# RWKV token-mix projections prepared one stream ahead, the gate as split products, and attention heads alternated on halves of the array

## The chip, the cores and the metric

One core of a Trainium2 chip runs the whole program. The metric is the device time of one execution in microseconds. Each version is run several times, and the median is compared. One execution of each is also recorded by the hardware profiler, and its trace is what the rows below come from.

## What is computed

The program is a block of a diffusion backbone over 512 latent and 256 context tokens, 1,024 channels wide. Two of its parts matter here. The first mixes tokens by neighbourhood attention, 64 channels a head:

```python
s_nb = einsum('bchd,bicjhd->bhcij', q_row, k_nb) * scale + bias
s_cx = einsum('bchd,bnhd->bhcn', q_row, k_ctx) * scale
p = softmax(concatenate([s_nb.reshape(...), s_cx], axis=-1), axis=-1)
...
return einsum('bhcij,bicjhd->bchd', p_nb, v_nb) + einsum('bhcn,bnhd->bchd', p[..., n_win:], v_ctx)
```

Context tokens attend to context tokens alone (`context_attention`). The second prepares an RWKV recurrence. Six streams are made of the tokens and of the mean of their neighbours, each by its own `mu`, and each has its own product:

```python
def rwkv_prepare(h, mu, w_rkv, w0, w1, w2, a0, a1, a2, g1, g2, k_k, k_a):
    xx = centred_shift(h) - h                 # 0.5 * (left + right) - h
    xr, xw, xk, xv, xa, xg = h[None] + xx[None] * mu[:, None, None, :]
    r, k, v = einsum('sbtd,sde->sbte', stack([xr, xk, xv]), w_rkv)
    w_logit = w0 + einsum(tanh(einsum('btd,zdr->zbtr', xw, w1)), w2)
    a = sigmoid(a0 + einsum(einsum('btd,zdr->zbtr', xa, a1), a2))
    g = sigmoid(xg @ g1) @ g2
    kk = k * k_k, each head divided by its norm
```

## The kernel before

Activations lie with channels on partitions: eight tiles of 128 channels by 768 tokens (512 latent, then 256 context). Large products run in float32r. `split` (L471) makes of a float32 tile a rounded part on ACT (L473) and the rest of it by a subtraction (L474, on DVE for activations, on POOL for weights, from `load_w`, L476). `dense` (L486, matmul at L495) then multiplies three pairs of parts for each of the eight input tiles k: hi·hi, hi weight by lo activation, lo weight by hi activation. A product of one block of 128 outputs is thus 24 matmuls of 512 columns and, where context is needed, 24 of 256. `dense_pair` (L499) interleaves the first two output blocks over k, so that a stream that is still being made feeds two blocks.

Every engine runs its instructions in one fixed order. A scheduler settles these orders when the program is built, from the order of the code, the data and the release of buffers. [...]

Attention (`na_attn`, L803) is a generator whose steps a written order (`AB_ORDER`) puts between dense products of the same mixer. One call does two heads, which lie on rows 0–63 and 64–127 of the same q and k tiles. It goes over six query blocks i (four latent ones against 512 keys, two context ones against 256) and, within each, over the two heads `hh`: the scores of a unit two further on (L820, L821), softmax (bias and maximum L778, L780, L781; exponent on ACT L785; L786, L787), transposes (L793) with a copy (L798), and the products with values `po` (L842), 64 columns of the array a head. Score, transpose and `po` banks come from one ring of four PSUM banks.

`rw_mixer` (L1105) makes the shifted tiles in `shift` (L1131: scaling on DVE L1135, bias on ACT L1137, the sum of neighbours on POOL L1138, two edge columns on POOL L1139, L1140). `stream(i, parts)` (L1144) makes all eight split tiles of stream i at once: xs (L1155), then `split`; for the first stream it also turns the neighbours' sum into xx, in place (L1151). Its tiles `ah`, `al` have eight buffers each, as many as one stream needs. `project` (L1161) does the products; `keep` (L1171) copies a result out on ACT (L1173) and writes it by DMA; `unit` (L1188) forms the normed k: a product `ssk` (L1192), a root on ACT (L1193), and on DVE L1194, a reciprocal (L1195) and L1196. The streams follow one another as k (2), v (3), w1 (1), a1 (4), r (0) and g1 (5); r and g1 have latent columns alone, w1 and a1 one output block, g1 two. After g1 come a sigmoid (L1227) and the gate: eight blocks of two float32 matmuls (L1230 with 128 rows, L1231 with 32 rows). Behind it the recurrence starts.

## Time and profile before

| | us |
|---|---|
| runs shown | 3583.0, 3583.03, 3589.97 |
| median | 3583.03 |
| the profiled execution, its own time | 3583.87 |
| its span, first to last instruction | 3581.7 |
| PE busy in the span | 3238.9 (90%) |
| DVE, ACT, POOL busy | 1791.7 (50%), 1312.9 (37%), 908.3 (25%) |
| mean granted clock of TensorE, share of full | 0.956 |

PE is the matrix engine, PEld its weight loads (they overlap it), DVE, ACT and POOL the vector, scalar and general engines, SP the engine that issues most DMAs. A busy share is an average over stages. What a change in one stage is worth is read from the rows of that stage. In a row of the timeline, the number behind an engine and line is a group of equal instructions (x8), `128*64` is the rows and columns of the array that a matmul uses, and a bracket gives the idle time before the group and what ended it. A float32 matmul leaves two records, a float32r one leaves one.

### The profile page before, as it was taken

To read this page: it belongs to the slowest core of one execution; us is meant where nothing else is said; L and a number is where in the kernel's file an instruction comes from. 1 tells how busy PE (TensorE), PEld (TensorE's weight loads), DVE (VectorE), ACT (ScalarE), POOL (GpSimd) and SP (SyncE) were. 2 spreads that over 40 slices of the span, in tenths; PEclk is the share of its full clock that TensorE was granted. 3 is DMA by queue.
4 is the path that set the end of the run, shared out by engine and by line. 5 is a ranking of instruction groups with operands and counts; after the bars stand their busy time and mean duration, and the time that the engine had idled before them with its cause. 6 is when DMAs were issued, how large, how long until landed. Compare 5 with 4: busy or idle time off the path is not lost. (4 is left out here: it accounts for less than half of the span.)

```text
span 3581.7 us, 56701 instructions
## 1 busy us (share of the span) xinstructions
PE 3238.9 (90%) x23582; PEld 2448.4 (68%) x23582; DVE 1791.7 (50%) x3066; ACT 1312.9 (37%) x2491; POOL 908.3 (25%) x468
## 2 busy tenths in 40 slices
PE   7999999999999798779999998899999989799887
PEld 4766887788888576467777776677778767433333
DVE  5475564862322655377777674574333564221213
ACT  3232353221212324367777775322233453200001
POOL 1111113322223522432222220444452333200000
PEclk9999999999999898789999999999999999899999
DMA  5212212552122232210000102475331236699997
GB/s 217 94 66 88 83 67 76 195 192 65 59 65 90 88 113 76 69 31 29 27 27 27 31 8 77 139 231 175 94 126 62 66 92 222 254 426 426 426 427 324
DMA packets 126225, 488.05 MB, mean 136 GB/s; under 512 B 13360, under 2 KB 23024, under 8 KB 101648
## 3 DMA queue, kind: packets, MB, share of 16 engines
q1 hardware_dynamic: 119840, 476.86, 36.9%
q8 instruction: 186, 3.05, 0.4%
q10 hardware_dynamic: 4944, 3.36, 0.3%
q0 software_dynamic: 1184, 4.20, 0.3%
q14 instruction: 71, 0.58, 0.0%
HBM read 455.53 MB, written 28.84 MB: 135 GB/s over the span
## 5 line engine op out<-in xcount | busy, mean ns | idle before, releaser
L474 POOL TENSOR_TENSOR wl<-w,wh 128x1024 fp32r<-128x1024 f32 (+1 forms) x258 | 616.8, 2393 | 1640.7 <-ACT wh L473 1444.6
L473 ACT ACTIVATE wh<-w 128x1024 fp32r<-128x1024 f32 (+1 forms) x258 | 265.9, 1032 | 944.1 <-PE dn L495 334.5
L495 PE MATMUL dn<-hh,wh 128*128 128x512 f32 (+1 forms) x768 | 236.1, 362 | 14.2 <-ACT hh L473 14.2
L495 PE MATMUL up<-ah,wl 128*128 128x512 f32 (+1 forms) x768 | 236.7, 363 | 6.4 <-POOL wl L474 6.3
L495 PE MATMUL up<-ah,wh 128*128 128x512 f32 (+1 forms) x768 | 236.9, 364 | 5.7 <-ACT ah L578 2.8
L495 PE MATMUL dn<-hl,wh 128*128 128x512 f32 (+1 forms) x768 | 236.4, 362 | 1.9 <-DVE hl L474 1.9
L495 PE MATMUL up<-al,wh 128*128 128x512 f32 (+1 forms) x768 | 236.5, 362 | 0.2 <-DVE al L579 0.2
L495 PE MATMUL dn<-hh,wl 128*128 128x512 f32 (+1 forms) x768 | 235.5, 361 | 0.9 <-POOL wl L474 0.9
L462 DVE SCALAR_TENSOR_TENSOR side<-wside,condb 128x1024 f32<-128x1024 f32 x128 | 191.9, 1499 | 67.6 <-DMA wside<-ada 66.3
L618 DVE TENSOR_TENSOR u<-u 128x768 f32<-128x768 f32 (+1 forms) x64 | 126.7, 1982 | 132.2 <-ACT u L617 132.2
L586 DVE SCALAR_TENSOR_TENSOR x<-dn,ada,x 128x512 f32<-128x512 f32 x96 | 60.5, 658 | 259.0 <-PE dn L495 259.0
L495 PEld LDWEIGHTS dn<-hh,wh 128*128 128x128 f32 x768 | 128.3, 190 | 39.8 <-ACT hh L473 15.8
L495 PEld LDWEIGHTS up<-ah,wl 128*128 128x128 f32 x768 | 128.5, 190 | 33.4 <-POOL wl L474 10.1
L495 PEld LDWEIGHTS up<-ah,wh 128*128 128x128 f32 x768 | 128.9, 191 | 31.4 <-ACT ah L578 3.9
L495 PEld LDWEIGHTS dn<-hl,wh 128*128 128x128 f32 x768 | 128.1, 190 | 27.4 <-DVE hl L474 3.8
L495 PEld LDWEIGHTS up<-al,wh 128*128 128x128 f32 x768 | 129.0, 191 | 25.2 <-DVE al L579 1.4
L495 PEld LDWEIGHTS dn<-hh,wl 128*128 128x128 f32 x768 | 128.2, 190 | 25.2 <-POOL wl L474 1.7
L495 PE MATMUL rp<-xh,wh 128*128 128x512 f32 x368 | 111.1, 373 | 23.3 <-ACT xh L473 21.5
L495 PE MATMUL rp<-xl,wh 128*128 128x512 f32 x368 | 113.5, 373 | 18.0 <-DVE xl L474 18.0
L473 ACT ACTIVATE hh<-u 128x768 fp32r<-128x768 f32 (+1 forms) x64 | 47.3, 739 | 219.4 <-DVE u L618 219.4
L495 PE MATMUL p<-ah,wh 128*128 128x512 f32 (+1 forms) x320 | 117.0, 394 | 2.2 <-ACT ah L578 1.2
L495 PE MATMUL p<-ah,wl 128*128 128x512 f32 x320 | 113.3, 383 | 2.1 <-POOL wl L474 2.1
(616 smaller groups left out, 7496.7 us busy)
## 6 DMA issues: line engine op xcount, KB each, us to landing
w<-mlp SPq DMA_DIRECT2D x128, 512.0 KB, 3.6
wside<-ada SPq DMA_DIRECT2D x96, 512.0 KB, 4.0
ew<-e_gate SPq DMA_DIRECT2D x45, 1024.0 KB, 19.5
ew<-e_up SPq DMA_DIRECT2D x41, 1024.0 KB, 20.7
ew<-e_down SPq DMA_DIRECT2D x39, 1024.0 KB, 19.5
wada<-ada SPq DMA_DIRECT2D x48, 512.0 KB, 3.8
ewm<-e_up SPq DMA_DIRECT2D x18, 1024.0 KB, 19.6
ewm<-e_down SPq DMA_DIRECT2D x18, 1024.0 KB, 19.6
```

Source lines behind the costliest of these rows:

```text
L462: nc.vector.scalar_tensor_tensor(o, w, 1.0, cb[:, q, :], op0=ALU.mult, op1=ALU.mult, accum_out=out[:, f, q:q + 1])
L473: nc.scalar.activation(hi, src, AF.Copy)
L474: (eng or nc.vector).tensor_tensor(lo, src, hi.bitcast(F32), op=ALU.subtract)
L495: nc.tensor.matmul(ps[:, a:b], ww[:, 128 * k:128 * k + 128], aa[:, a:b], start=(first and k == 0 and q == 0), stop=(last and k == nk - 1 a ...
L586: self.nc.vector.scalar_tensor_tensor(x[:, a:b], ps[:, a:b], gt[:, f, q:q + 1], x[:, a:b], op0=ALU.mult, op1=ALU.add)
L618: nc.vector.tensor_tensor(u[:, lo:hi], u[:, lo:hi], u[:, lo:hi], op=ALU.mult)
```

## The change

**Streams.** `stream` becomes a generator `tiles` in an object `Stream`. `ah` and `al` get 14 buffers (`NX`), so up to six tiles of the next stream can exist beside the eight of the present one. `ahead()` makes one of them behind each product but the first of a long stream; ahead of w1 and a1, which have one product, six tiles of the stream that follows are made in one go. w1 now follows k and precedes v. For the first stream xx is not written: ACT makes h·(1−mu) and DVE adds mu/2 times the neighbours' sum; the writing of xx is moved to the second stream. The first tile's neighbours' sum goes from POOL to DVE.

**Gate.** The sigmoid's result is split; `g2` is loaded and split like other weights. The 32 last rows are stacked three times, so that one matmul of 96 rows does their three products. Each block of the gate is four float32r matmuls in place of two float32 ones.

**Attention.** The scores of both heads of a query block are issued alternately, as are their `po` products, and the scores of the next block go between the two transposes.

```diff
-    o["rw_g1"] = chunk_w(v["rw_g1"][0])
-    o["rw_g2"] = np.ascontiguousarray(v["rw_g2"][0])
+    g1, g2 = v["rw_g1"][0], v["rw_g2"][0]
+    o["rw_g1"] = chunk_w(np.concatenate([g1] + [g1[:, 128:]] * 2, 1))
+    o["rw_g2"] = np.stack([g2[:128], np.concatenate([g2[128:]] * 3 + [np.zeros((32, D), g2.dtype)])])
+NX = 14
...
+                def scores(i):
+                    s = [self.bank("s"), self.bank("s")]
+                    for j in range(2 if i < 4 else 1):
+                        for hh in range(2):
+                            r = slice(64 * hh, 64 * hh + 64)
+                            a = 128 * i if i < 4 else T + 128 * (i - 4)
+                            kj = k[r, 8 * win[i]:8 * win[i] + 256] if i < 4 and j == 0 else k[r, T:]
+                            nc.tensor.matmul(s[hh][:, 256 * j:256 * j + 256], q[r, a:a + 128], kj, start=True, stop=True)
+                    return s
+                s = scores(0)
+                for i in range(6):
+                    pT, s2 = [], None
+                    for hh in range(2):
+                        if i < 4:
+                            pr, w = softmax(s[hh], bias[hh][:, i, :], 512), 512
+                            vs = (win[i] // 8, win[i] // 8 + 2, 7, 8)
+                        else:
+                            pr, w = softmax(s[hh], None, 256), 256
+                            vs = (7, 8)
+                        if hh and i < 5:
+                            s2 = scores(i + 1)
+                        pT.append(p_t(pr, w))
+                        if hh == 0:
+                            yield
+                    s = s2
+                    po = self.bank("po")
+                    for j, v in enumerate(vs):
+                        for hh in range(2):
+                            r = slice(64 * hh, 64 * hh + 64)
+                            nc.tensor.matmul(po[r, :128], vt[:, v, r], pT[hh][:, 128 * j:128 * j + 128],
+                                             start=(j == 0), stop=(j == len(vs) - 1))
                     if i < 4:
...
                         nc.vector.tensor_copy(
                             cat[f][:, :T].rearrange("p (r c) -> p c r", r=8)[:, 16 * i:16 * i + 16, :],
                             po[:, :128].rearrange("p (c r) -> p c r", r=8))
...
+                    else:
                         a = T + 128 * (i - 4)
                         nc.scalar.activation(cat[f][:, a:a + 128], po[:, :128], AF.Copy)
                     yield
@@ -1135,28 +1138,51 @@
                         nc.vector.scalar_tensor_tensor(h[:, a:b], self.x[k][:, a:b], sc[:, k, q:q + 1], r[q],
                                                        op0=ALU.mult, op1=ALU.mult)
                         nc.scalar.activation(h[:, a:b], h[:, a:b], AF.Identity, bias=sh[:, k, q:q + 1])
-                        nc.gpsimd.tensor_tensor(s[:, a + 1:b - 1], h[:, a:b - 2], h[:, a + 2:b], op=ALU.add)
+                        (nc.gpsimd if k else nc.vector).tensor_tensor(s[:, a + 1:b - 1], h[:, a:b - 2], h[:, a + 2:b], op=ALU.add)
                         nc.gpsimd.tensor_copy(s[:, a:a + 1], h[:, a + 1:a + 2])
                         nc.gpsimd.tensor_copy(s[:, b - 1:b], h[:, b - 2:b - 1])
-                def stream(i, parts):
+                m2 = pool.tile([128, 2, 8], F32, name="mu2", bufs=1)
+                nc.vector.tensor_scalar(m2[:, 0, :], self.p("mu")[:, 16:24], 0.5, None, op0=ALU.mult)
+                nc.vector.tensor_scalar(m2[:, 1, :], self.p("mu")[:, 16:24], -1.0, 1.0, op0=ALU.mult, op1=ALU.add)
+                def tiles(i, parts, out):
                     lo, hi = parts[0][0], parts[-1][1]
-                    out = []
                     for k in range(KD):
                         while len(xx) < min(k + 3, KD):
                             shift(len(xx))
+                        t = pool.tile([128, TT], F32, tag="tmp", name=self.uid("xs"), bufs=self.tb)
+                        h = pool.tile([128, TT], F32R, tag="ah", name=self.uid("xh"), bufs=NX)
+                        l = pool.tile([128, TT], F32R, tag="al", name=self.uid("xl"), bufs=NX)
+                        base, mu = hs[k], self.p("mu")[:, 8 * i + k:8 * i + k + 1]
                         if i == 2:
+                            nc.scalar.activation(t, hs[k], AF.Copy, scale=m2[:, 1, k:k + 1])
+                            base, mu = t, m2[:, 0, k:k + 1]
+                        elif i == 1:
                             nc.vector.scalar_tensor_tensor(xx[k], xx[k], 0.5, hs[k], op0=ALU.mult, op1=ALU.subtract)
-                        t = pool.tile([128, TT], F32, tag="tmp", name=self.uid("xs"), bufs=self.tb)
-                        h = pool.tile([128, TT], F32R, tag="ah", name=self.uid("xh"), bufs=KD)
-                        l = pool.tile([128, TT], F32R, tag="al", name=self.uid("xl"), bufs=KD)
-                        nc.vector.scalar_tensor_tensor(t[:, lo:hi], xx[k][:, lo:hi], self.p("mu")[:, 8 * i + k:8 * i + k + 1],
-                                                       hs[k][:, lo:hi], op0=ALU.mult, op1=ALU.add)
+                        nc.vector.scalar_tensor_tensor(t[:, lo:hi], xx[k][:, lo:hi], mu, base[:, lo:hi],
+                                                       op0=ALU.mult, op1=ALU.add)
                         self.split(t[:, lo:hi], h[:, lo:hi], l[:, lo:hi])
                         out.append((h, l))
-                    return out
+                        yield
+                class Stream:
+                    def __init__(st, i, parts):
+                        st.act = []
+                        st.gen = tiles(i, parts, st.act)
+                    def step(st, n=KD):
+                        for _ in range(n):
+                            next(st.gen, None)
+                        return st.act
+                    def ahead(st):
+                        if len(st.act) < NX - KD:
+                            st.step(1)
-                act = stream(2, PARTS)
+                streams = {i: Stream(i, LAT if i in (0, 5) else PARTS) for i in (2, 1, 3, 4, 0, 5)}
+                act = streams[2].step()
                 self.x = None
                 def unit(f, t, sq):
                     for a, b in PARTS:
@@ -1204,31 +1232,52 @@
                     if late:
                         late()
                     late = partial(unit, f, t, sq)
-                act = stream(3, PARTS)
+                    if f > 0:
+                        streams[1].ahead()
+                act = streams[1].step()
+                streams[3].step(NX - KD)
+                for f, ps in project(act, self.i["rw_w1"], 1, PARTS):
+                    factors(tw, ps, AF.Tanh)
+                act = streams[3].step()
+                late()
                 for f, ps in project(act, self.i["rw_v"], KD, PARTS):
                     keep("v", f, ps, 0, TT)
-                    if late:
-                        late = late()
-                act = stream(1, PARTS)
-                for f, ps in project(act, self.i["rw_w1"], 1, PARTS):
-                    factors(tw, ps, AF.Tanh)
-                act = stream(4, PARTS)
+                    if f > 0:
+                        streams[4].ahead()
+                act = streams[4].step()
+                streams[0].step(NX - KD)
                 for f, ps in project(act, self.i["rw_a1"], 1, PARTS):
                     factors(ta, ps, AF.Copy)
-                act = stream(0, LAT)
+                act = streams[0].step()
                 for f, ps in project(act, self.i["rw_r"], KD, LAT):
                     keep("r", f, ps, 0, T)
-                act = stream(5, LAT)
-                tg = pool.tile([128, 2, T], F32, name="tg", bufs=1)
-                g2 = pool.tile([128, 2, D], F32, name="g2", bufs=1)
-                nc.sync.dma_start(g2[:, 0, :], self.i["rw_g2"][:128])
-                nc.sync.dma_start(g2[:32, 1, :], self.i["rw_g2"][128:])
+                    if f > 0:
+                        streams[5].ahead()
+                act = streams[5].step()
+                def part(tag):
+                    return pool.tile([128, TT], F32R, tag=tag, name=self.uid("tg"), bufs=NX)[:, :T]
+                th, tl, tx = part("ah"), part("al"), part("ah")
                 for f, ps in project(act, self.i["rw_g1"], 2, LAT):
-                    nc.scalar.activation(tg[:, f, :], ps[:, :T], AF.Sigmoid)
+                    t = pool.tile([128, TT], F32, tag="tmp", name=self.uid("tg"), bufs=self.tb)[:, :T]
+                    nc.scalar.activation(t, ps[:, :T], AF.Sigmoid)
+                    if f == 0:
+                        self.split(t, th, tl)
+                    else:
+                        nc.scalar.activation(tx[:96], t[:96], AF.Copy)
+                        nc.vector.tensor_tensor(tx[32:64], t[32:64], tx[32:64].bitcast(F32), op=ALU.subtract)
+                g2 = self.load_w(self.i["rw_g2"][0], D)
+                w = self.wraw.tile([128, D], F32, tag="wraw", name=self.uid("w"))
+                nc.sync.dma_start(w, self.i["rw_g2"][1])
+                gx = self.wspl.tile([128, D], F32R, tag="wh", name=self.uid("wh"))
+                nc.scalar.activation(gx[:96], w[:96], AF.Copy)
+                nc.vector.tensor_tensor(gx[64:96], w[64:96], gx[64:96].bitcast(F32), op=ALU.subtract)
                 for f in range(KD):
                     pg = self.bank("g")
-                    nc.tensor.matmul(pg, g2[:, 0, 128 * f:128 * f + 128], tg[:, 0, :], start=True, stop=False)
-                    nc.tensor.matmul(pg, g2[:32, 1, 128 * f:128 * f + 128], tg[:32, 1, :], start=False, stop=True)
+                    c = slice(128 * f, 128 * f + 128)
+                    for n, (w, t) in enumerate(((g2[0], th), (g2[0], tl), (g2[1], th), (gx[:96], tx[:96]))):
+                        nc.tensor.matmul(pg, w[:, c], t, start=(n == 0), stop=(n == 3))
                     keep("g", f, pg, 0, T)
             self.close_w()
```

Lines move: L793 becomes L796, L798 L801, L820 and L821 L822, L842 L845, `dense` L498, `split` L476 and L477, L1155 L1167, L1194 to L1196 L1222 to L1224, L1227 L1264, L1173 L1199.

PE in the attention of the first mixer; `pqkv` is a dense product that the written order puts between, `s` scores, `pt` transposes, `po` products with values. Before:

```order
L793 MATMUL pt_769<-consts,p_765 128x128 x4
L495 MATMUL pqkv_873<-ah_303,wl_877 128x256
L495 MATMUL pqkv_873<-ah_312,wh_876 128x512
L495 MATMUL pqkv_873<-ah_312,wh_876 128x256
L495 MATMUL pqkv_873<-al_313,wh_876 128x512
L495 MATMUL pqkv_873<-al_313,wh_876 128x256
L495 MATMUL pqkv_873<-ah_312,wl_877 128x512
L842 MATMUL po_753<-pT_774,vt_709 64x128 x4
L820 MATMUL s_781<-qk_483,qk_478 128x256
L821 MATMUL s_781<-qk_483,qk_478 128x256
L793 MATMUL pt_792<-consts,p_788 128x128 x4
```

After:

```order
L796 MATMUL pt_789<-consts,p_785 128x128 x4
L822 MATMUL s_804<-qk_483,qk_478 128x256
L822 MATMUL s_805<-qk_483,qk_478 128x256
L822 MATMUL s_804<-qk_483,qk_478 128x256
L822 MATMUL s_805<-qk_483,qk_478 128x256
L796 MATMUL pt_810<-consts,p_800 128x128 x4
L845 MATMUL po_817<-pT_794,vt_709 64x128
```

and, behind six dense ones:

```order
L845 MATMUL po_817<-pT_815,vt_709 64x128
L845 MATMUL po_817<-pT_794,vt_709 64x128
L845 MATMUL po_817<-pT_815,vt_709 64x128
L845 MATMUL po_817<-pT_794,vt_709 64x128
L845 MATMUL po_817<-pT_815,vt_709 64x128
```

The scores of two banks now alternate and stand between two transposes, and `po` of the two heads alternates (seven of its eight matmuls stand behind six dense ones); dense matmuls between are as many per head as they were.

DVE from the last products of k to the stream that follows; `sqk` is `unit`'s tile, `xs` and `xl` are tiles of streams. Before:

```order
L1196 SCALAR_TENSOR_TENSOR sqk_9894<-keep_9891,params,sqk_9894 128x768
L1155 SCALAR_TENSOR_TENSOR xs_10046<-xx_9352,params,x_4575 128x768
L1155 SCALAR_TENSOR_TENSOR xs_10052<-xx_9363,params,x_4576 128x768
L1194 TENSOR_SCALAR sqk_9964<-sqk_9964 128x768
L474 TENSOR_TENSOR xl_10048<-xs_10046,xh_10047 128x768
L1195 RECIPROCAL sqk_9964<-sqk_9964 128x768
L474 TENSOR_TENSOR xl_10054<-xs_10052,xh_10053 128x768
L1196 SCALAR_TENSOR_TENSOR sqk_9964<-keep_9961,params,sqk_9964 128x768
```

After:

```order
L1167 SCALAR_TENSOR_TENSOR xs_10091<-xx_9449,params,x_4581 128x768
L1222 TENSOR_SCALAR sqk_10002<-sqk_10002 128x768
L1223 RECIPROCAL sqk_10002<-sqk_10002 128x768
L477 TENSOR_TENSOR xl_10093<-xs_10091,xh_10092 128x768
L1224 SCALAR_TENSOR_TENSOR sqk_10002<-keep_9999,params,sqk_10002 128x768
L1167 SCALAR_TENSOR_TENSOR xs_10098<-xx_9467,params,x_4582 128x768
L1167 SCALAR_TENSOR_TENSOR xs_10105<-xx_9355,params,x_4575 128x768
L1167 SCALAR_TENSOR_TENSOR xs_10111<-xx_9366,params,x_4576 128x768
L477 TENSOR_TENSOR xl_10100<-xs_10098,xh_10099 128x768
L477 TENSOR_TENSOR xl_10107<-xs_10105,xh_10106 128x768
```

Before, the new stream's first tiles stand here, behind two `unit`s. After, these are its seventh and eighth tile (`xs_10091`, `xs_10098`), and the tiles behind them belong to the stream after it; the reciprocal of a `unit` stands ahead of the low part `xl_10093`.

ACT at the gate; `tg` is the sigmoid, `wh` the rounded part of weights. Before:

```order
L473 ACTIVATE xh_11143<-xs_11142 128x512
L473 ACTIVATE xh_11149<-xs_11148 128x512
L1227 ACT_TABLE_LOAD
L1227 ACTIVATE tg<-rp_11170 128x512
L1227 ACTIVATE tg<-rp_11171 128x512
L1173 ACTIVATE keep_11225<-g_11222 128x512
```

After:

```order
L476 ACTIVATE xh_11160<-xs_11159 128x512
L476 ACTIVATE wh_11240<-w_11238 128x1024
L1264 ACT_TABLE_LOAD
L1264 ACTIVATE tg_11230<-rp_11180 128x512
L1264 ACTIVATE tg_11234<-rp_11181 128x512
L476 ACTIVATE tg_11165<-tg_11230 128x512
L1268 ACTIVATE tg_11167<-tg_11234 96x512
L1274 ACTIVATE wh_11246<-w_11244 96x1024
L1199 ACTIVATE keep_11254<-g_11249 128x512
```

A rounding of weights (`wh_11240`) now stands ahead of the table load, and three roundings between the sigmoids and the first copy out of the gate.

## Rows read from the trace of the kernel before

**Rows 1.** Busy time by windows, attention between dense products (columns in the first line).
```profile
core 0: us, PE busy (x) PEld busy (x) DVE busy (x) ACT busy (x) POOL busy (x), PEclk, DMA share, GB/s
95.00:147.00 52.00, 51.78 (x300) 35.96 (x299) 29.57 (x82) 17.24 (x35) 7.21 (x3) 1.00 0.33 112
```

**Rows 2.** Timeline of PE, one unit (start, us, group).
```profile
102.95 1.09 PE L842 MATMUL po<-pT,vt 128*64 128x128 f32 x8
103.97 0.70 PE L820 MATMUL s<-qk,qk 64*128 64x256 f32 x2
...
105.03 0.66 PE L793 MATMUL pt<-consts,p 128*128 128x128 f32 x4
...
106.66 1.09 PE L842 MATMUL po<-pT,vt 128*64 128x128 f32 x8
```

**Rows 3.** Timeline of DVE, the same place.
```profile
105.72 0.69 DVE L798 COPY pT<-pt 128x512 f32<-128x512 f32 x1
...
110.62 0.48 DVE L787 TENSOR_SCALAR p<-p,smx 128x512 f32<-128x512 f32 x1
```

**Rows 4.** Timeline of PE, other places where matmuls use parts of the array.
```profile
2799.26 0.46 PE L2192 MATMUL go<-gS,qh 64*64 64x128 f32 x4
2799.48 0.46 PE L2187 MATMUL kv<-vt,kt 64*64 64x128 f32 x4
...
3539.49 0.59 PE L2290 MATMUL eu<-ew,xT 128*64 128x512 f32 x1
3539.50 0.59 PE L2290 MATMUL eu<-ewa,xT 128*64 128x512 f32 x1
```

**Rows 5.** Busy time by windows, the RWKV projections (columns as in rows 1).
```profile
1185.00:1200.00 15.00, 11.37 (x40) 8.43 (x40) 15.00 (x18) 7.07 (x12) 15.00 (x22) 0.71 0.00 0
...
1186.20:1222.70 36.50, 26.32 (x100) 19.79 (x101) 27.46 (x30) 14.38 (x21) 25.98 (x37) 0.80 0.03 11
...
1280.80:1312.00 31.20, 23.59 (x107) 17.87 (x105) 27.13 (x22) 12.92 (x18) 4.99 (x3) 0.89 0.18 69
1312.00:1361.30 49.30, 49.30 (x284) 43.30 (x284) 3.06 (x3) 8.96 (x11) 14.26 (x6) 1.00 0.37 130
1361.30:1377.40 16.10, 12.01 (x49) 9.42 (x48) 13.74 (x15) 8.20 (x11) 2.37 (x1) 0.79 0.16 59
1377.40:1396.80 19.40, 11.28 (x49) 8.48 (x48) 18.39 (x19) 11.12 (x14) 2.96 (x1) 0.82 0.09 27
1396.80:1416.70 19.90, 15.03 (x52) 10.80 (x51) 12.49 (x17) 10.97 (x16) 4.86 (x3) 0.83 0.14 50
1416.70:1450.10 33.40, 32.39 (x142) 26.48 (x142) 2.25 (x3) 8.88 (x12) 14.19 (x7) 1.00 0.35 120
1450.10:1465.30 15.20, 12.98 (x48) 10.04 (x48) 11.62 (x23) 6.95 (x11) 6.46 (x4) 0.89 0.05 17
1465.30:1482.30 17.00, 16.99 (x34) 4.78 (x33) 1.06 (x4) 4.81 (x9) 1.41 (x2) 1.00 0.28 105
```

**Rows 6.** Waits of PE from 1178 to 1482: us in total, times, longest.
```profile
PE rp L495 <- ACT xh L473: 21.5, 10, 7.6
PE rp L495 <- DVE xl L474: 18.0, 15, 3.5
PE ssk L1192 <- ACT sqk L1203: 2.3, 2, 1.3
```

**Rows 7.** Timeline of the first streams, PE and DVE.
```profile
1191.53 0.95 DVE L1151 SCALAR_TENSOR_TENSOR xx<-xx,x 128x768 f32<-128x768 f32 x1
...
1211.74 1.01 PE L495 MATMUL rp<-xl,wh 128*128 128x512 f32 x2 [3.50 <-DVE xl L474]
...
1285.35 4.94 DVE L1195 RECIPROCAL sqk<-sqk 128x768 f32<-128x768 f32 x1
```

**Rows 8.** Timeline around the start of the gate.
```profile
1460.01 1.28 ACT L1227 ACT_TABLE_LOAD   x1
...
1464.73 1.28 ACT L1227 ACTIVATE tg<-rp 128x512 f32<-128x512 f32 x2 [3.44 <-PE rp L495]
...
1465.38 1.12 PE L1230 MATMUL g<-tg,g 128*128 128x512 f32 x2
```

More of the change, by code (lines that the diff above doesn't have):

```diff
@@ L809, in na_attn @@
                     bias.append(bt)
-                units = [(i, hh) for i in range(6) for hh in range(2)]
-                s, po = {}, None
-                def scores(u):
-                    i, hh = u
-                    r = slice(64 * hh, 64 * hh + 64)
-                    s[u] = self.bank("s")
-                    if i < 4:
-                        qi = q[r, 128 * i:128 * i + 128]
-                        nc.tensor.matmul(s[u][:, :256], qi, k[r, 8 * win[i]:8 * win[i] + 256], start=True, stop=True)
-                        nc.tensor.matmul(s[u][:, 256:], qi, k[r, T:], start=True, stop=True)
-                    else:
-                        a = T + 128 * (i - 4)
-                        nc.tensor.matmul(s[u][:, :256], q[r, a:a + 128], k[r, T:], start=True, stop=True)
@@ L826, in na_attn @@
-                for u in units[:2]:
-                    scores(u)
-                for n, (i, hh) in enumerate(units):
-                    r = slice(64 * hh, 64 * hh + 64)
-                    if n + 2 < 12:
-                        scores(units[n + 2])
-                    if i < 4:
-                        pr, w = softmax(s.pop((i, hh)), bias[hh][:, i, :], 512), 512
-                        vs = (win[i] // 8, win[i] // 8 + 2, 7, 8)
-                    else:
-                        pr, w = softmax(s.pop((i, hh)), None, 256), 256
-                        vs = (7, 8)
-                    pT = p_t(pr, w)
-                    if hh == 0:
-                        po = self.bank("po")
-                    for j, v in enumerate(vs):
-                        nc.tensor.matmul(po[r, :128], vt[:, v, r], pT[:, 128 * j:128 * j + 128],
-                                         start=(j == 0), stop=(j == len(vs) - 1))
-                    if hh == 1 and i < 4:
+                def scores(i):
[7 more added lines that the diff above has]
+                    return s
@@ L847, in na_attn @@
                             po[:, :128].rearrange("p (c r) -> p c r", r=8))
-                    elif hh == 1:
+                    else:
                         a = T + 128 * (i - 4)
```

## The prediction

> **What bounds the kernel now.** I read the windows first, because the change touches two stretches and the average over the whole program says nothing of either. In the attention stretch PE is busy 51.78 of 52.00 us at full clock [rows 1]: what leaves PE there leaves the time, as long as no other engine becomes late. In the RWKV projections the picture alternates. The inner part of a stream is pure PE (49.30 of 49.30 for six blocks of v, so 8.2 us a block; 33.40 for six blocks of r, 5.6 us each), but every change of stream is not: 31.20 us with PE 23.59 at v, 16.10 with 12.01 at w1, 19.40 with 11.28 at a1, 19.90 with 15.03 at r, 15.20 with 12.98 at g1 [rows 5]. The granted clock is 0.79 to 0.89 in them, a mix of its two levels, 2.4 and 1.2 GHz, against 1.00 inside the streams. The waits name the cause: PE stood 21.5 us for rounded activations and 18.0 us for their low parts [rows 6]. The first pair of k is another case: in its first 15 us DVE and POOL are both busy all the time [rows 5].
>
> **Attention.** One unit takes 106.66 − 102.95 = 3.71 us, so a latent query block with its two heads takes 7.42 us. Of it 2 × 1.06 us are scores (103.97 to 105.03) and 2 × 1.02 us are `po` (102.95 to 103.97, eight records, 0.127 us a record) [rows 2]. The change issues two heads' matmuls on opposite halves alternately. The nearest rows for what that is worth are two. `go` and `kv`, 64 rows by 64 columns, begin four records every 0.22 us, 0.055 us a record. Two `eu` matmuls on column halves begin 0.01 us apart and take 0.59 us each [rows 4], while one float32 record of the same 512 columns that uses all columns takes 0.56 us (two in 1.12) [rows 8]. So halves do run side by side. No row has row halves with all columns, as the scores now have; I take them as the others, since `go` and `kv` differ in rows too. Scores then cost 1.06 us a block instead of 2.12, and `po` about 0.95 (one record pair ahead of the dense matmuls, the rest at 0.055) instead of 2.04. PE's work falls to 7.42 − 1.06 − 1.09 = 5.3 us.
>
> PE will not get all of it. The order shows the second head's transposes directly behind the scores. Between the two sets of transposes DVE must copy the first (0.69 us) and scale the second head (0.48 us) [rows 3], 1.17 us and two hand-overs against 1.06 us of scores: a wait of some 0.5 us. Behind the second set, DVE has the maxima of the new scores in front of the copy that `po` needs, with six dense matmuls as cover: another 0.4 us. That makes 6.2 us a block, 1.2 us less. Four calls have 16 latent blocks: 19 us. The 8 context blocks have half the scores and half the `po`, 1.0 us to win and the same waits: 0.4 us each, 3 us. **Sum 22 us.** Ends: no waits, 16 × 2.15 + 8 × 1.0 = 42 us; no overlap on the array with 0.5 us of waits left, 16 × 0.5 = 8 us lost.
>
> One rule speaks against half of this. The Trainium skill (TensorE: Matmul & The Clock Gate, Part 3: Packing small matmuls) says that a weight load overlaps matmuls in flight only where the two use different row groups. The heads' `po` matmuls use different columns but the same 128 rows, so by that rule their loads would stand between them. The trace speaks against such a cost for the matmuls as a whole: those of `eu`, also on all 128 rows, begin 0.01 us apart [rows 4].
>
> **First pair of k.** DVE does five instructions a tile there (18 in 15.00 us, so 4.2 us a tile), POOL six (22, 4.1 us) [rows 5]. The change takes the writing of xx, 0.95 us [rows 7], off DVE for each of eight tiles and gives ACT, 7.07 us busy of 15, one scaling more. It takes the first tile from POOL, the first thing everybody waits for. POOL then sets about 3.5 us a tile. Eight tiles at 0.7 us less are 5.6 us, and the start is about 1.5 us earlier: **7 us**. Ends: 3 us, if POOL's pace stays, and 10 us, if it follows DVE. The eight writings of xx come back in the same order on DVE behind k's last tile, 7.6 us, beside the 16 us that the pair's matmuls take; if that cover went, they would delay `unit` alone, whose result goes to memory.
>
> **Changes of stream.** Against 8.2 and 5.6 us a block, the five windows hold 31.2 − 16.4 = 14.8, 16.1 − 8.2 = 7.9, 19.4 − 8.2 = 11.2, 19.9 − 11.2 = 8.7 and 15.2 − 11.2 = 4.0 us too much, together 46.6 us [rows 5], of which rows 6 explain most as waits and the lowered clock the rest. About 5 us stay whatever happens: the last `unit`'s `ssk` and its wait (2.3 us with the one before [rows 6]), and the third block's weights. With six of eight tiles ready, the seventh and eighth are the next to be late. At the change from k to w1 the order puts them on DVE behind a `unit`: PE's last product, root, L1222, a reciprocal of 4.94 us [rows 7], then a low part, L1224 and three xs before the last low part. That is about 13 us after k's end, by my estimate (hand-over and root 2.4, the reciprocal, and six operations of about 1 us [rows 7]), where w1 wants it after 7.2: some 5.5 us late. The other changes have no `unit` in front except v, whose last tiles stand behind the same chain: 3.5 us more. **46.6 − 5 − 9 = 33 us.** Waits like these have been followed by the lower clock (the 3.50 us wait at 1211.74 stands in the window of clock 0.80 [rows 5, 7]), so I take **3 us off**.
>
> What DVE gains in work inside k: one tile of the next stream a block, xs and low part, 1.9 us, beside 6.6 us of `unit` (4.94 and two lighter passes of at most 1 us [rows 7]). 8.5 us fit in the 8.2 us of products plus `ssk`, about 9.6 us a block, barely. In v only 2 us are added to an idle DVE (3.06 us busy in 49.30 [rows 5]). The SP queue keeps its order, with w1's weights ahead of v's and the gate's weights behind g1's.
>
> **Gate.** 17.00 us now [rows 5]. 32 float32r matmuls at 33.40 / 6 / 24 = 0.23 us are 7.4 us. In front of them ACT now rounds weights, loads its table (1.28 us, before hidden behind g1's matmuls, 1460.01), then two sigmoids (1.28) and one rounding (0.64, a sigmoid's time): 4.5 us with 1.3 us for the weights, where 0.65 us passed before (1464.73 to 1465.38) [rows 8]. The fourth matmul of the first block waits for the stacked weights, two roundings on, 2 us. 4.5 + 2 + 7.4 = 14 against 17.6: **3 us**, between 0 and 6. The copies out of the gate and all that waits for them move along.
>
> **Sum.** 22 + 7 + 33 − 3 + 3 = 62 us, against the profiled execution's 3583.87: 3521.9, so 3522. The median of the runs, 3583.03, is 0.02% below that execution. About 0.2% (7 us) is what a measurement of this kernel can tell from no change.
>
> **Rivals.**
> - *The loads of `po` do not overlap.* Then a block saves the scores' 1.06 us less about 0.8 us of waits, 4 us over all, 2 more in context blocks: 62 − 22 + 6 = 46, 3538. For it: no row shows these loads with equal rows in so short a matmul (128 columns); against it: `eu`.
> - *Attention gives nothing, or loses up to 8 us*, because the DVE chain (PE waits for two DVE steps in a row where before one head's dense matmuls stood between) takes what the array gives: 40 us left, 3544, to 3552. For it: DVE was busy 29.57 of 52.00 us [rows 1] and its work is now in two bursts.
> - *The look-ahead holds half.* 8.5 of 9.6 us on DVE leave it no slack; if `unit` falls behind, tiles come as late as before, and a tile's buffer returns late. 62 − 20 = 42: 3542.
> - *Slower: the clock falls in the attention.* If the idle time in a block grows to the 3.5 us of the wait at 1211.74, PE may be granted 1.2 GHz through the dense matmuls between heads. 177 us of attention (48 units of 3.71) at half clock for about 60% of the time cost 100 us: 3620. It decides from waits of that length on; I see 0.5 us, a seventh.
> - *Nothing changes.* The order shows the new sequence in the program, so only equal and opposite effects could do it: 3584.
>
> **Chances.** Forecast 0.52, loads 0.10, attention nothing 0.18, half 0.14, clock 0.03, no change 0.03. The first four are all faster by over 0.2%: 0.94; same 0.03; slower 0.03. The forecast's own ends (7 us from the first pair, 6 from the gate, 15 from attention, 10 from the streams, not all on one side) give 3498 to 3537; the next three reach 3552. The range is 3498 to 3552.
>
> **What would show it.** In attention: `po` and scores groups of half the time, a block of about 6.2 us, waits of PE on L801 and L790 new in the list. In the projections: windows at the five changes near 8.2 or 16.4 us with clock 1.00, except w1 and v; waits on xh and xl from 39.5 down to about 12 us. At the gate: PE idle some 4 us, then 8 us of matmuls. The prediction is wrong if the attention's score rows keep 0.265 us a record (1.06 us for four), if DVE is busy through k and PE still waits in w1 for over 8 us, or if the granted clock sinks where PE was full.

## The result, and the profile after

The changed kernel takes 3540.24 us (median of four runs, 3538.09 to 3541.96) against 3583.89 (four runs). The ratio is 0.9879, 95% interval 0.9865 to 0.9893: 43.7 us faster, where 62 were forecast. The time lies in the range, the sign was right, and the size was seven tenths of the forecast. The time alone does not say which mechanism held: 3540 lies nearer to three of the rivals (3538, 3542 and 3544) than to the forecast of 3522. The stages have to decide.

The starts and ends of the same work in the two traces show where the time went. Each line is a group of PE's matmuls that both kernels have:

| | before | after | shift | new in this step | forecast |
|---|---|---|---|---|---|
| first product of k | 1186.25 | 1167.80 | −18.45 | −18.5 (attention) | −22 |
| first `ssk`, behind the first pair of k | 1221.50 | 1196.40 | −25.10 | −6.6 (first pair) | −7 |
| start of the last matmul of g1 | 1464.99 | 1419.35 | −45.64 | −20.5 (changes of stream) | −30 |
| end of the gate | 1482.31 | 1430.89 | −51.42 | −5.8 (gate) | −3 |
| first `d` of the recurrence | 1517.05 | 1470.13 | −46.92 | +4.5 | 0 |
| end of the last `comb` of the program | 3565.80 | 3523.92 | −41.88 | +5.0 | 0 |

The timeline of PE after shows two ends of attention blocks and their waits (start, us, group, idle time before):

```profile
105.12 0.63 PE L796 MATMUL pt<-consts,p 128*128 128x128 f32 x4 [1.96 <-DVE p L790]
105.67 0.43 PE L845 MATMUL po<-pT,vt 128*64 128x128 f32 x2
...
107.29 1.09 PE L845 MATMUL po<-pT,vt 128*64 128x128 f32 x14
...
109.99 1.13 PE L822 MATMUL s<-qk,qk 64*128 64x256 f32 x8
111.53 0.63 PE L796 MATMUL pt<-consts,p 128*128 128x128 f32 x4 [0.40 <-DVE p L790]
```

Eight score records take 1.13 us, about what four of one head took [rows 2]; 14 records of `po` take 1.09, as eight did [rows 2]. The block between the two rows of `pt` takes 111.53 − 105.12 = 6.41 us, forecast 6.2. PE's waits in that mixer have one new line (us in total, times, longest). Two lines of the kernel before, 4.1 us ahead of the same transposes, are gone:

```profile
PE pt L796 <- DVE p L790: 11.6, 16, 2.0
```

Windows of the projections after, with bounds at the first matmul of each group (columns as in rows 1): first pair of k, the other six blocks, w1, pair of v, six blocks of v, a1, pair of r.

```profile
1167.80:1197.60 29.80, 24.11 (x100) 18.57 (x101) 28.02 (x30) 19.89 (x28) 23.61 (x37) 0.82 0.04 14
1197.60:1256.40 58.80, 58.44 (x315) 48.67 (x313) 58.45 (x30) 25.15 (x37) 16.75 (x8) 1.00 0.39 137
1256.40:1273.20 16.80, 12.55 (x54) 9.28 (x53) 16.73 (x14) 6.44 (x10) 2.31 (x1) 0.83 0.28 102
1273.20:1296.60 23.40, 19.54 (x99) 16.28 (x97) 23.08 (x20) 11.54 (x14) 3.32 (x2) 0.90 0.08 28
1296.60:1349.00 52.40, 51.24 (x289) 44.46 (x290) 19.25 (x14) 14.88 (x19) 16.44 (x7) 1.00 0.36 129
1349.00:1357.40 8.40, 8.40 (x50) 7.32 (x49) 6.02 (x8) 5.54 (x9) 2.42 (x1) 1.00 0.32 110
1357.40:1370.80 13.40, 11.78 (x50) 8.71 (x48) 10.95 (x13) 7.30 (x11) 3.38 (x2) 1.00 0.12 40
```

The same bounds in the kernel before, w1, pair of v, a1:

```profile
1363.70:1381.20 17.50, 11.99 (x49) 9.42 (x49) 17.50 (x17) 9.57 (x12) 3.79 (x2) 0.80 0.14 54
1283.70:1310.20 26.50, 20.73 (x98) 16.54 (x97) 25.56 (x21) 8.47 (x12) 0.72 (x1) 0.87 0.10 35
1381.20:1399.00 17.80, 11.32 (x49) 8.49 (x49) 15.72 (x19) 9.55 (x13) 1.34 (x2) 0.79 0.09 29
```

a1 is the picture of what was meant: 17.80 us became 8.40, PE without a gap at full clock. w1 is not: 17.50 became 16.80. There, and through the six blocks of k ahead of it and the pair of v behind it, DVE is busy all the time (58.45 of 58.80, 16.73 of 16.80, 23.08 of 23.40).

Part of that is POOL's weight split. In six blocks of k one DVE instruction with two input tiles stands beside it, took 2.3 to 3.2 us in place of 0.9 to 1.0, and ended 0.8 us behind the split:

```profile
1236.96 2.40 POOL L477 TENSOR_TENSOR wl<-w,wh 128x1024 fp32r<-128x1024 f32 x1 [7.28 <-PE ssk L1220]
1237.85 2.32 DVE L477 TENSOR_TENSOR xl<-xs,xh 128x768 fp32r<-128x768 f32 x1
```

So a block of k costs DVE 58.45 / 6 = 9.7 us, not the 8.5 of the prediction. No run here moves the splits away from there.

### The profile page after: what moved, and what is told of

It reads as the page before. It is cut to its first block, busy times and chain, and to the rows that moved or that the text cites. A ratio compares the mean times of both kernels' runs of the same rounds, so it can differ in the third digit from the quotient of the medians.

```text
span 3540.1 us, 56694 instructions
## 1 busy us (share of the span) xinstructions
PE 3200.3 (90%) x23582; PEld 2423.1 (68%) x23582; DVE 1822.3 (51%) x3073; ACT 1321.4 (37%) x2503; POOL 910.1 (26%) x467
## 5 line engine op out<-in xcount | busy, mean ns | idle before, releaser
L477 POOL TENSOR_TENSOR wl<-w,wh 128x1024 fp32r<-128x1024 f32 (+1 forms) x259 | 623.5, 2410 | 1614.1 <-ACT wh L476 1461.6
L476 ACT ACTIVATE wh<-w 128x1024 fp32r<-128x1024 f32 (+1 forms) x259 | 266.9, 1032 | 920.3 <-PE dn L498 335.6
L498 PE MATMUL dn<-hh,wh 128*128 128x512 f32 (+1 forms) x768 | 236.4, 362 | 15.1 <-ACT hh L476 15.1
L498 PE MATMUL up<-ah,wh 128*128 128x512 f32 (+1 forms) x768 | 236.9, 364 | 6.5 <-ACT ah L581 2.8
L498 PE MATMUL up<-ah,wl 128*128 128x512 f32 (+1 forms) x768 | 236.6, 362 | 6.1 <-POOL wl L477 5.9
L498 PE MATMUL dn<-hl,wh 128*128 128x512 f32 (+1 forms) x768 | 236.7, 362 | 2.2 <-DVE hl L477 2.2
L498 PE MATMUL dn<-hh,wl 128*128 128x512 f32 (+1 forms) x768 | 235.8, 361 | 1.1 <-POOL wl L477 1.1
L498 PE MATMUL up<-al,wh 128*128 128x512 f32 (+1 forms) x768 | 236.6, 362 | 0.2 <-DVE al L582 0.2
L498 PEld LDWEIGHTS dn<-hh,wh 128*128 128x128 f32 x768 | 128.5, 190 | 40.4 <-ACT hh L476 16.6
L498 PEld LDWEIGHTS up<-ah,wh 128*128 128x128 f32 x768 | 128.9, 191 | 32.5 <-ACT ah L581 3.9
L498 PEld LDWEIGHTS up<-ah,wl 128*128 128x128 f32 x768 | 128.3, 190 | 33.3 <-POOL wl L477 9.9
L498 PEld LDWEIGHTS dn<-hl,wh 128*128 128x128 f32 x768 | 128.4, 190 | 28.0 <-DVE hl L477 4.3
L498 PEld LDWEIGHTS up<-al,wh 128*128 128x128 f32 x768 | 129.0, 191 | 25.2 <-DVE al L582 1.4
L498 PEld LDWEIGHTS dn<-hh,wl 128*128 128x128 f32 x768 | 128.3, 190 | 25.7 <-POOL wl L477 2.0
L476 ACT ACTIVATE hh<-u 128x768 fp32r<-128x768 f32 (+1 forms) x64 | 47.3, 740 | 220.1 <-DVE u L621 220.1
L498 PE MATMUL p<-ah,wh 128*128 128x512 f32 (+1 forms) x320 | 118.7, 400 | 2.2 <-ACT ah L581 1.2
L498 PE MATMUL rp<-xl,wh 128*128 128x512 f32 x368 | 110.2, 364 | 10.2 <-DVE xl L477 10.2
L498 PE MATMUL rp<-xh,wh 128*128 128x512 f32 x368 | 110.1, 366 | 9.1 <-ACT xh L476 7.8
L498 PE MATMUL p<-ah,wl 128*128 128x512 f32 x320 | 113.6, 384 | 2.1 <-POOL wl L477 2.1
```

Source lines behind the costliest of these rows:

```text
L476: nc.scalar.activation(hi, src, AF.Copy)
L477: (eng or nc.vector).tensor_tensor(lo, src, hi.bitcast(F32), op=ALU.subtract)
L498: nc.tensor.matmul(ps[:, a:b], ww[:, 128 * k:128 * k + 128], aa[:, a:b], start=(first and k == 0 and q == 0), stop=(last and k == nk - 1 a ...
```

## The experiments

All ratios are to runs of the kernel before on the same chip (0.9879 for the changed kernel). Its medians there lie between 3581.8 and 3584.2 us, so a difference between two of the times below is good to a few us; where the stages of the traces say more, they are given.

**Each part alone.** *Attention alone* is the kernel before with the new `na_attn`.

> The kernel before with the attention part of the change alone. The trace of the changed kernel lost 18.4 us of PE's time by the end of the first mixer and nothing of it came back up to the RWKV projections. Theory (the parts add up): 18 us faster than before, 16 to 20, a latent block near 6.4 us. Rival (time won early is lost again behind, by transfers or the clock): under 10 us.

Measured: 3565.85 against 3581.81, ratio 0.9947 (0.9930 to 0.9963): 16.0 us, at the low end of the theory. Its first product of k starts at 1172.42, 13.8 us earlier than before. The same product starts at 1165.96 to 1169.78 in the six traces whose code is the changed kernel's up to there, and at 1184.42 to 1186.25 in the three with the old attention. So what attention is worth is known to a few us. *Streams alone*:

```diff
+                tg = [pool.tile([128, TT], F32, tag="ah", name=self.uid("tg"), bufs=NX)[:, :T] for _ in range(2)]
...
+                g2 = [self.wraw.tile([128, D], F32, tag="wraw", name=self.uid("g2")) for _ in range(2)]
```

> The kernel before with the streams part alone: old attention, gate in float32 from tiles held in other buffers. Theory (ledger of the trace): 6.6 us from the first pair of k and 20 us from the changes of stream, together 25 to 28 us faster than before, and nothing lost behind the gate, so that it alone gives more than streams and gate together did in the changed kernel (23.5 us behind the attention). Rival (the loss behind the gate does not come from the gate): 20 to 23 us.

3555.92, ratio 0.9922 (0.9906 to 0.9939): 25.9 us, inside the theory's numbers. *Gate alone*, with eight buffers for its tiles as before:

> The kernel before with the gate part alone. Theory: the gate ends about 6 us earlier, but the memsets on POOL behind it, 14.4 us that the first products of the recurrence wait for, start at the release of a buffer that the last copies of the gate hold, 3 us behind the gate's end instead of 1.4 us ahead of it; 1 to 2 us remain. Rival (what the gate wins is carried through): 5 to 6 us faster than before.

3582.33 against 3581.81, ratio 0.9999 (0.9989 to 1.0009): nothing to be measured. POOL in its trace shows why:

```profile
1475.56 1.51 POOL L1299 MEMSET kd<- 128x1536 f32 x1 [6.38 <-DMA d_g<-keep]
...
1490.81 1.26 POOL L476 TENSOR_TENSOR l2l<-y,l2h 128x512 fp32r<-128x512 f32 x1
```

In the kernel before the same two stand at

```profile
1480.89 1.38 POOL L1284 MEMSET kd<- 128x1536 f32 x1 [17.39 <-ACT keep L1173]
...
1495.25 1.26 POOL L474 TENSOR_TENSOR l2l<-y,l2h 128x512 fp32r<-128x512 f32 x1
```

The shorter gate ends earlier, but the memsets then wait for the transfer of the gate's copies, and the low part `l2l` of the recurrence's first weights stands behind them on POOL. The three parts alone, 16.0 + 25.9 − 0.5 = 41.4 us, add up to the whole, 43.7, within the noise.

**The halves of the array.**

```diff
-                    for j, v in enumerate(vs):
-                        for hh in range(2):
+                    for hh in range(2):
+                        for j, v in enumerate(vs):
```

> The changed kernel with the products po of one head behind those of the other, at the same place; scores still alternate. Theory (column halves run side by side only when they alternate; the trace of the changed kernel shows 14 records of po in 1.09 us where eight took 1.09): a latent block gets about 0.7 us longer, 16 blocks and half as much in 8 others, 12 to 14 us slower than the changed kernel, less what hides in the wait for DVE; 8 to 14. Rival (DVE's chain holds the block anyway): under 3 us slower.

In PE's timeline of this run `po` is back at its old rate:

```profile
104.74 1.09 PE L845 MATMUL po<-pT,vt 128*64 128x128 f32 x8
...
106.31 1.09 PE L845 MATMUL po<-pT,vt 128*64 128x128 f32 x8
```

Here dense products stand between the two heads. Where none does, five times in the first mixer, all sixteen records take 1.94 us, no less than two times eight one behind the other; so on the same rows being neighbours is not enough:

```profile
127.13 1.94 PE L845 MATMUL po<-pT,vt 128*64 128x128 f32 x16
```

The first product of k starts at 1178.69 in place of 1167.80, 10.9 us later, as expected (traces of one code differ by up to 3.8 us there). The whole run gives less, 3546.28, ratio 0.9893 (0.9873 to 0.9913), 6 us of median; its later stages ran faster than the changed kernel's, which no part of the edit touches (the recurrence's own spread is given further below). The same exchange of loops in `scores`:

> The changed kernel with the scores of one head behind those of the other, at the same place between the transposes; po still alternates. Theory (row halves run side by side only when they alternate): eight score records take 2.1 us in place of 1.1, but they lie where PE waits 0.4 us for the copy and the scaling on DVE anyway; 0.6 us a latent block, 8 to 12 us slower than the changed kernel. Rival (order within the two heads does not matter, or the wait hides it all): under 3 us.

3541.65, ratio 0.9876 (0.9856 to 0.9896): the rival holds for the time. And the scores did not get slower at all:

```profile
109.65 1.14 PE L822 MATMUL s<-qk,qk 64*128 64x256 f32 x8
```

Eight records take 1.14 us with one head's four behind the other's in the program. In this trace they begin in pairs, 0.013 us apart (109.652 and 109.665, 109.972 and 109.985, and so on): the second head's matmuls start beside the first head's and not behind them. So the row halves run side by side when the two heads' scores are neighbours, alternated or not; the theory falls. (The mixer was 8 us longer by k's first product, 1175.96; a dense matmul had slipped between the scores and the transposes, and PE stood at half clock for 20.5 us there in place of 10.2. How much is the edit's and how much chance was not tried.)

**Scaling on ACT**, on top of the two edits further below:

```diff
+                if act:
+                    nc.scalar.activation(pr[:, :n], pr[:, :n], AF.Copy, scale=m[:, 3:4])
...
```

> The two edits of the run before last (norming deferred, low part of the recurrence's first weights on DVE) and a third: the second head's probabilities are scaled on ACT in place of DVE. Theory (PE's 11 us of waits ahead of the second head's transposes, 15 or 16 of them, come from DVE doing the first head's copy and the second head's scaling one behind the other): the scaling runs beside the copy, most of these waits go, 6 to 11 us faster than with the two edits, 74 to 79 faster than before. Rival (the exponent itself, or the reciprocal, is late, or ACT is held up by its other work): under 2 us.

3516.44, ratio 0.9812 (0.9795 to 0.9829), the same as without it: the rival holds. PE's waits ahead of the transposes are 10.4 us in place of 11.6. DVE's queue in this run shows what was overlooked: the reciprocal that the scaling needs stands behind the copy, and starts 1.7 us after the exponent that it reads was done (107.89).

```profile
109.00 0.69 DVE L804 COPY pT<-pt 128x512 f32<-128x512 f32 x1 [1.00 <-PE pt L799]
109.61 0.15 DVE L789 RECIPROCAL smx<-smx 128x1 f32<-128x1 f32 x1
```

**The first pair.** xx written in the first stream again (`if i == 2` as in the kernel before, without ACT's scaling):

> The changed kernel with xx written again in the first stream (on DVE, as in the kernel before) and no scaling on ACT. Theory (DVE and POOL set the pace of the first pair, and taking xx off DVE there is what won the 6.6 us): the pair gets 4 to 6 us longer, and the change to w1 does not get shorter, since the writing lay under the pair's products: 4 to 6 us slower than the changed kernel. Rival (POOL alone sets the pace, and the 6.6 us came from the first tile's sum on DVE): under 2 us slower.

From the first product of k to the first `ssk` it took 1202.35 − 1169.46 = 32.9 us in place of 28.6: 4.3 us of the 6.6 are xx's. What the other 2.3 us are was not tested. The whole is 3542.27, ratio 0.9884 (0.9865 to 0.9902), 2 us slower and not clear of the noise; the stage decides for the theory.

**The change from k over w1 to v.** First the order:

```diff
+                    if f == KD - 1:
+                        streams[1].step()
                     if late:
                         late()
```

> The changed kernel with one edit: the seventh and eighth tile of w1's stream are made ahead of the last but one unit of k. Theory (PE's 7.6 us of waits in w1 and the 5 us of half clock behind them come from the reciprocal that stands ahead of these tiles on DVE): w1's waits go, 4 to 8 us of it return at the start of v, whose tiles now stand behind that reciprocal; 4 to 9 us faster than the changed kernel, so 46 to 51 faster than before. Rival (POOL's splits of weights slow DVE there, whatever the order): under 2 us faster than the changed kernel.

3537.65, ratio 0.9868 (0.9851 to 0.9884): 2.6 us less, not clear of the noise. In its trace w1 takes 13.5 us in place of 16.8 and the pair of v 27.0 in place of 23.4: what w1 won, v lost, and the theory's 4 to 9 us are not there. That spoke for the amount of DVE's work, not its order. Two runs tested it:

> The changed kernel without the reciprocal in unit, eight of 4.95 us on DVE: kk is multiplied by the norm (scaled down) where it should be divided by it, so this leaves a part of the computation out and only prices it. Theory (DVE's total work between the last blocks of k and the first of v, not the order in it, bounds the change from k over w1 to v): all waits of PE on tiles there go with their half clock, 10 to 13 us faster than the changed kernel. Rival (POOL's weight splits, which lock DVE, or ACT set these waits): under 4 us.

3526.43, ratio 0.9837 (0.9814 to 0.9860): 14 us faster than the changed kernel. In the traces, 8.4 us of it lie between w1's first matmul and g1's last (154.6 us in place of 163.0). w1 takes 9.7 in place of 16.8, as the theory has it. But the pair of v keeps waits and takes 24.1 in place of 23.4, though DVE is busy for only 16.87 us there:

```profile
1266.51:1290.59 24.08, 20.51 (x99) 17.04 (x97) 16.87 (x17) 10.79 (x15) 3.64 (x2) 0.86 0.10 38
```

PE stands 1.9 us for a rounded tile and 1.2 us for a low part, and half clock follows. Three xs on DVE took 5.01 us there, beside a split of 2.96 us on POOL, and 2.87 some us earlier without one. So the reciprocals are not all of it. And with all work kept, but the norming of the last three units behind blocks of v:

```diff
+                    if f < KD - 3:
+                        norm(f, t, sq)
+                    else:
+                        nc.sync.dma_start(spill["kk"][f], sq)
...
                     keep("v", f, ps, 0, TT)
+                    if 0 < f < 4:
+                        norm_back(KD - 4 + f)
```

> The changed kernel with the norming of the last three units of k moved behind the second to fourth block of v, where DVE has 2 us of work in 8: their roots go to memory and come back with k. Theory (DVE bounds the change from k to w1 to v): the same waits go, 8 to 12 us faster than the changed kernel, and v does not slow down. Rival (other engines set the waits, or the transfers delay v's blocks): under 3 us faster, or slower.

3520.84, ratio 0.9824 (0.9803 to 0.9845): 63 us faster than before, 20 more than the changed kernel, 15.4 of them between w1's first matmul and g1's last. The windows of w1, pair of v and six blocks of v in its trace:

```profile
1254.50:1264.20 9.70, 9.70 (x54) 8.12 (x53) 6.97 (x9) 7.23 (x11) 2.50 (x2) 1.00 0.41 137
1264.20:1281.80 17.60, 17.11 (x98) 14.72 (x96) 13.42 (x13) 10.11 (x14) 3.35 (x2) 1.00 0.26 74
1281.80:1333.20 51.40, 50.62 (x288) 44.11 (x289) 37.83 (x23) 15.25 (x19) 16.83 (x7) 1.00 0.52 187
```

w1 takes 9.70 in place of 16.80 and the pair of v 17.60 in place of 23.40: 12.9 us, at full clock. DVE's busy time in v's six blocks rises from 19.25 to 37.83 us and costs nothing there. What DVE had to do from the end of k to v's pair was the bound: 39.8 us in w1 and the pair of v in the changed kernel, 24.3 without the reciprocals and 20.4 with the norming deferred, and only with the last do no waits for tiles stay. How much of the rest is POOL's splits is not shown.

**Behind the gate.**

```diff
-            self.split(raw, wh.rearrange("p n m -> p (n m)"), wl.rearrange("p n m -> p (n m)"), nc.gpsimd)
+            self.split(raw, wh.rearrange("p n m -> p (n m)"), wl.rearrange("p n m -> p (n m)"), nc.gpsimd if f else nc.vector)
```

> The changed kernel with the low part of the recurrence's first weights made on DVE, which is idle there, in place of POOL, where it stands behind 14.4 us of memsets. Theory (behind the gate the memsets on POOL are the path, so most of what the gate wins is lost there): the first products of the recurrence with that low part start up to 8 us earlier and 4 to 8 us of it reach the end. Rival (the recurrence waits for transfers or for the buffers that the memsets clear): under 2 us.

3530.88, ratio 0.9846 (0.9827 to 0.9865): 9 us better than the changed kernel by median, with single runs from 3522.77 to 3535.51. The traces are steadier. From the gate's end to the first `d` pass 34.6 to 34.7 us in the three with the old gate, 36.4 to 39.2 in the eight with the new gate and this low part on POOL, and 30.6 to 31.3 in the three with it on DVE. In PE's timeline the product with the low part follows the one with the rounded part at once:

```profile
1442.98 0.79 PE L1501 MATMUL b<-tw,l2h 128*128 128x512 f32 x1 [9.11 <-ACT l2h L476]
1443.70 0.79 PE L1501 MATMUL b<-tw,l2l 128*128 128x512 f32 x1
```

where the changed kernel waited:

```profile
1440.43 1.01 PE L1501 MATMUL b<-tw,l2h 128*128 128x512 f32 x2 [9.30 <-ACT l2h L476]
1449.65 0.79 PE L1501 MATMUL b<-tw,l2l 128*128 128x512 f32 x1 [8.21 <-POOL l2l L477]
```

So the queue on POOL took back what the gate had won. Both edits together:

> The two edits together: norming of the last three units behind blocks of v, and the low part of the recurrence's first weights on DVE. Theory (they are in different places and add up): 20 us from the first as measured and 4 to 8 from the second, 24 to 28 us faster than the changed kernel, 67 to 72 faster than before. Rival (one path behind both): as fast as the first edit alone, 63 us faster than before.

3516.23 against 3584.05, ratio 0.9809 (0.9793 to 0.9826): 67.8 us faster than before, at the low end of the theory. This version beats both kernels.

## Why the prediction was right or wrong

- **Attention, 22 forecast, 18.5 by the trace.** The mechanism held: both kinds of halves run side by side. That the numbers are so near is in part luck, because two terms were off and cancel. The array gave 30.3 us of PE's busy time, not the 42 of the forecast's full overlap. The windows of the mixer show `po` before and after, then the scores before and after; PE's busy time stands behind the length:

```profile
95.00:380.00 285.00, 45.32 (x320) 33.74 (x320) 6.08 (x16) 2.22 (x8) 0.98 0.23 78
95.00:380.00 285.00, 32.56 (x320) 21.22 (x320) 6.20 (x16) 2.22 (x8) 0.98 0.23 82
95.00:380.00 285.00, 43.38 (x172) 25.45 (x172) 33.14 (x80) 34.39 (x98) 0.98 0.23 78
95.00:380.00 285.00, 25.87 (x172) 15.25 (x172) 31.20 (x80) 34.35 (x98) 0.98 0.23 82
```

In `po`, 0.37 us for the first two records (105.67 to the dense matmul at 106.04) and 1.01 for the other 14 make 1.38 us a block, not 0.95. Against the array's gain the forecast set 20 us, and the trace shows 12. They are 11.6 us of new waits less the 4.1 that are gone, and a term that was put at nothing. Before, four transposes held PE for 0.41 us, since dense matmuls followed; now scores or `po` follow, on parts of the array, and they hold it for 0.53 us (109.46 to 109.99). Counted from start to start, all transposes of that mixer take 22.5 us in place of 16.6.

```profile
105.03 0.66 PE L793 MATMUL pt<-consts,p 128*128 128x128 f32 x4
105.44 0.37 PE L495 MATMUL pqkv<-ah,wl 128*128 128x256 f32 x1
```

```profile
109.46 0.60 PE L796 MATMUL pt<-consts,p 128*128 128x128 f32 x4
```

The working had a slip as well: in a context block, 1.0 us to win less the same 0.9 us of waits leaves 0.1, not 0.4. The rival on weight loads falls: column halves on the same rows run side by side when the heads alternate, and the run with `po` head by head prices that at 10.9 us. So the rule of the Trainium skill (TensorE: Matmul & The Clock Gate, Part 3: Packing small matmuls) does not hold this matmul back. The rivals "nothing" and "the clock falls" did not come.
- **First pair, 7 forecast, 6.6.** Right in sum, not in its parts: the start came no earlier (from the last `pml` matmul of the mixer ahead to the first product of k both kernels take 692 us, so that product's shift is attention's), and the pair itself won more. The 3.5 us a tile for POOL, from which the 5.6 us came, stood in no row.
- **Changes of stream, 33 − 3 forecast, 20.5: the step that failed.** Two terms of it. *"About 5 us stay whatever happens"* was about 10: so much is left with nearly all waits for tiles gone, in the run with deferred norming. The pair of r still takes 13.5 us against 11.2 of pure blocks, the pair of v 17.6 against 16.4, w1 9.7 against 8.2 and g1 12.6 against 11.2, 6.4 us together; the six blocks of v and of r hold another 3.2 (51.4 against 49.2, 34.6 against 33.6). PE's waits for low weights (3.9 us) and for copies (1.3) and the matmuls of `ssk` are in that. *"46.6 − 5 − 9"*: the 9 us of new delay, with 3 for the clock, were 12.9 us in w1 and the pair of v alone, and 15.4 between `ssk` and g1's end. I had counted the chain behind k's end, a reciprocal and six operations, and called DVE's 8.5 of 9.6 us a block a fit. It was 9.7: the instruction beside POOL's weight split was counted at its length alone. The windows show 58.45 of 58.80: DVE was full, the units were behind when k ended, and the queue did not empty until v's pair was over. The rival "the look-ahead holds half" had this mechanism, at 3542.
- **Gate, 3 forecast, 5.8 at its end and 1.3 behind.** The start cost 3.2 us (forecast 3.9) and the wait for the stacked weights did not come. "The copies out of the gate and all that waits for them move along" was the wrong step: memsets that wait for those copies' transfers, and a weight part behind them, took 4.5 us back (2 to 4.5 over the eight traces).
- **The rest, +5.0,** was not forecast, and is no loss that the change can be charged with. From the first `d` to the last `comb` the code is the same in all fourteen traces, and they take 2043.3 to 2053.8 us; the kernel before has 2048.8, the changed kernel is the longest. What makes this stretch vary was not tried. The total times above hold this spread too.

## What to carry to other kernels

Work that is moved ahead to hide a wait lands on an engine's queue: add up that engine's busy time over the stretch, not only the length of the one chain at its end, and with what another engine's work adds to its instructions. Where the engine is full, as DVE was here with 58.45 of 58.80 us, the wait only moves. Then look for the next stretch in which that engine is idle, and defer work without a near reader to it. And follow a shortened stage to its first reader, through the buffers that its copies hold: behind the gate, memsets waited for a transfer, not for the gate.

## What the hardware showed that was not expected

- Two heads' scores on opposite row halves overlap when they are neighbours in PE's queue, alternated or not: 1.13 and 1.14 us for eight records. Counted to the next matmul's start, eight take 1.07 (109.65 to 110.72 in the run with one head behind the other) and four of one head 1.06 [rows 2]. `po`, on column halves of the same rows, overlaps only when it alternates: 14 records in 1.09 us, 16 head by head in 1.94.
- A DVE instruction can wait for a weight split on POOL inside its own length. In the changed kernel the scaling of 512 columns, 0.49 us elsewhere, took 1.81 while POOL split weights from 102.34 on, and ended 0.28 us behind the split. Not every instruction does: the reciprocal at 1201.92 took its usual 4.94 us, though a split ran from 1201.70 to 1204.27.

```profile
103.16 1.81 DVE L790 TENSOR_SCALAR p<-p,smx 128x512 f32<-128x512 f32 x1
```

```profile
102.34 2.35 POOL L477 TENSOR_TENSOR wl<-w,wh 128x1024 fp32r<-128x1024 f32 x1 [10.51 <-ACT wh L476]
```

PE's wait of 1.96 us at 105.12 is this one. The Trainium skill (SBUF — State Buffer, SBUF: two separate sides) states it as a lock that one of the two engines holds for a whole instruction; the trace agrees, with 1.81 against 0.49.
